# Bidirectional gated DeltaNet encoder: k and q of one chunk as one stationary matrix, and the layouts that follow

## The chip, the cores and the metric

The kernel runs on one core of one Trainium2 chip. The metric is the device time of one execution in microseconds, from the chip. One more execution was recorded by the hardware profiler; its times are those of the profile below.

## The reference, cut to what matters

One encoder layer of width 2048 over two sequences of 256 tokens in float32: h + W_out [ neighbourhood attention, 8 heads; bidirectional gated DeltaNet, 8 heads ](RMSNorm(h)), then a SwiGLU block, then a last RMSNorm. The change is in the DeltaNet heads. A sequence is cut into four chunks of 64 tokens, and a state S (128x128) runs over the chunks, once forward and once backward:

```python
def step(S, inp):
    q_i, k_i, u_i, w_i, g_i, qk_i = inp
    v_new = u_i - jnp.einsum('bhcd,bhde->bhce', w_i, S)
    o = jnp.einsum('bhcd,bhde->bhce', q_i * jnp.exp(g_i)[..., None], S) \
        + jnp.einsum('bhcs,bhse->bhce', qk_i, v_new)
    g_last = g_i[..., -1]
    S = S * jnp.exp(g_last)[..., None, None] + jnp.einsum(
        'bhcd,bhce->bhde', k_i * jnp.exp(g_last[..., None] - g_i)[..., None], v_new)
    return S, o
...
o = o_fwd + o_bwd
o = o * lax.rsqrt(jnp.mean(o * o, axis=-1, keepdims=True) + RMS_EPS) * norm_w.astype(jnp.float32)
```

u and w come from a triangular solve inside the chunk. The kernel writes a step with one matrix for each chunk and direction: r = v - exp(g) (k S), n = U r (U is the solved matrix), o = exp(g) (q S) + QK n, and S' = S exp(g_last) + kd' n, with kd the k rows scaled by their decay.

## The kernel before, in words

Both sequences lie side by side as 512 columns. All large products are 128x128 by 128x512. Weights are split into a high and a low part (load_w, L143 to L150: SP loads w_raw at L146 into one of three buffers, ScalarE makes w_hi at L138, VectorE w_lo at L139), and each product is three matmuls (mm3). half_gemm (L197 on) does eight such triples with one weight load and, after every second triple (six large matmuls, a "pump"), advances the generators in two lists, chains and side. These generators hold everything else: convolutions, attention, the lanes and the recurrence. `yield from pause(n)` lets n pumps pass. Matmuls and transposes are kept in program order; the other engines' instructions are put in order by a scheduler.

The DeltaNet heads pass through these steps:

- **k and q** (loop over 8 heads, L616 to L635): projection, convolution and silu give kq, [128 dims, k or q, 512 tokens]. POOL stores it as s_kq (L634), and the products k k and q k of each chunk as s_gram.
- **lanes** (L502 to L614): the 128 (direction, chunk, head, sequence) combinations lie on 128 partitions, W is solved on VectorE (L590, L592), the scaled matrices are made (L604, L607), and POOL stores them as s_uq in eight stores of 512 KB (L612). row_factors (L526 to L552) transposes the per-token factors and ScalarE copies them into tables (L545, L548, L551): scs for kd, egk for r, egq for os, rqs for the last norm.
- **open_recurrence** (L738 to L749) opens the pool dr in the space of the lanes, and POOL clears four uq tiles (L746).
- **fetch** (L755 to L765) loads for one head s_kq on SP (L759, tile kq) and four pieces of s_uq on POOL (L762), into block-diagonal 128x128 matrices: forward in rows and columns 0 to 63, backward in the others, one for each sequence.
- **prepare** (L767 to L789) transposes v and k on TensorE into token rows, and VectorE scales k to kd (L786).
- **recur** (L791 to L859): one generator for a head, two together for a pair. Four stages; in stage st the forward direction does chunk st and the backward one chunk 3 - st. A stage has these blocks on TensorE, for both heads of the pair one after the other:
  - S,kq (stages 1 to 3): k and q of a chunk, 64 stationary columns each, times S: eight products of 128x64 by 128x128 a head. VectorE makes r (L815, 128 partitions, two a head); ScalarE makes os from the q part (L822), VectorE in stage 2 (L820).
  - r,uq (dvn,uq in stage 0): two products of 128x128 by 128x128 a head; ScalarE copies the result to n (L829).
  - n,kd and the update of S (L849), in stages 0 to 2; then O, eight 64x64 products a pair, into two PSUM tiles that stay for the whole pair (n,uq in the profile).
  - S_GAP, R_GAP and N_GAP (3, 2 and 2 pumps) lie between them.
- **finish_pair** (L874 to L912): os plus O (L871), the norm, transposes back, the product with the gate (yo, L909) and the split into dmix (L142), which goes into the W_out projection.

The names in the profile: kkq is the lanes' big tile, ev_* are evacuated projections, cacc is the convolution's sum, dvT its result, dvn v in token rows.

Of the kernel before, what the change touches and what calls it, by code (L numbers as in the profile page):

```python
# [18 lines left out]
P = 128  # L19
# [3 lines left out]
H = 8  # L23
# [51 lines left out]
def hybrid_encoder(ctx: ExitStack, tc: tile.TileContext, xT, w_in, w_ba, w_out, w_gate,  # L75
# [51 lines left out]
    s_kq = dp.tile([H, P, 2, T], F32, name="s_kq")  # L127
# [277 lines left out]
    scs, egk = tab[:, 0], tab[:, 1]  # L405
    egq = wk.tile([P, 8, H], F32, tag="egq", name="egq")
    rqs = wk.tile([P, 2, 2, H], F32, tag="rqs", name="rqs")
# [94 lines left out]
    def lanes():  # L502
# [23 lines left out]
        def row_factors():  # L526
            _, rq = norms(qq, "nq")
            yield
            rqd = vec("rqd", 2 * C)
            for i in range(2):  # L530
                ts(rqd[:, i * C:i * C + C], rq, QSCALE, None, ALU.mult)
            egd = vec("egd", 4 * C)
            for i in range(2):
                stt(egd[:, i * C:i * C + C], eg, -1.0, rk, ALU.mult, ALU.mult)
                nc.vector.tensor_copy(egd[:, (2 + i) * C:(3 + i) * C], eg)
            ps = sm_tile()
            mm(ps[:, :P], ones, dg, start=True, stop=True)
            nc.scalar.copy(egl, ps[:, :P])
            yield
            ps = sm_tile()  # L540
            for i, v in enumerate((kd, egd[:, :2 * C], egd[:, 2 * C:], rqd)):
                transpose(ps[:, i * P:i * P + P], v, ident)
            p2 = ps[:, :2 * P].rearrange("p (i l) -> p i l", i=2)
            for (hf, st), l0 in LN.items():
                nc.scalar.copy(tab[half[hf], :, st], p2[half[hf], :, l0:l0 + 16])  # L545
            qs = ps[:, 2 * P:].rearrange("p (k h b) -> p k h b", h=H, b=NB)
            for b in range(NB):
                nc.scalar.copy(egq[half[b]], qs[half[b], :8, :, b])  # L548
                for pp in range(2):
                    ks = slice(8, 12, 3) if pp == 0 else slice(9, 11)  # L550
                    nc.scalar.copy(rqs[half[b], pp], qs[half[b], ks, :, b])  # L551
            yield  # L552
# [63 lines left out]
    for h in range(H):  # L616
# [17 lines left out]
        nc.gpsimd.dma_start(s_kq[h], kq)  # L634
# [103 lines left out]
    def open_recurrence():  # L738
# [4 lines left out]
        UQ = []  # L743
        for i in range(4):
            u = dr.tile([P, 4, 2, P], F32, tag=f"uq{i}", name=f"uq{i}")
            nc.gpsimd.memset(u, 0.0)  # L746
            UQ.append(u)
# [7 lines left out]
    def fetch(h):  # L755

        uq = state["UQ"][2 * (h % 2):2 * (h % 2) + 2]
        kq = wk.tile([P, 2, T], F32, tag="kq", bufs=2, name="kq2")
        nc.sync.dma_start(kq, s_kq[h])  # L759
        for b in range(NB):  # L760
            for hf in range(2):
                nc.gpsimd.dma_start(  # L762
                    uq[b][half[hf], :, :, hf * C:hf * C + C].rearrange("s i w c -> s (i w) c"),
                    s_uq[h * NB + b, hf].rearrange("s i w c -> s (i w) c"))
        fetched[h] = uq, kq  # L765

    def prepare(h, vT):  # L767
# [6 lines left out]
        uq, kq = fetched[h]  # L774
        yield from pause(3 + h % 2)
        pv, pk = sm_tile(), sm_tile()
        for t, u in ((pv, vT), (pk, kq[:, 0])):
            for i in range(4):
                transpose(t[:, i * P:i * P + P], u[:, i * P:i * P + P], ident)
# [3 lines left out]
        pk4 = pk.rearrange("p (b q d) -> p b q d", b=NB, q=2)  # L783
        for st in range(3):
            pp = 0 if st in (0, 3) else 1
            tt(kd[:, st], pk4[:, :, pp],  # L786
               scs[:, st, h * NB:h * NB + NB, None].broadcast_to([P, NB, P]), ALU.mult)
        prepared[h] = (uq, kq, vn, kd)
        yield  # L789

    def recur(h, O):  # L791
        dr = state["dr"]
        uq, kq, vn, kd = prepared[h]
        os_ = na.tile([P, 2, NB, P], F32, tag="bias", bufs=2, name="os")
        S = None
        for st in range(4):
            pp = 0 if st in (0, 3) else 1

            dirs = (0, 1) if st < 2 else (1, 0)
            if S is None:  # L800
                rv = vn[:, :, pp]
            else:
                yield from pause(S_GAP)

                pks = sm_tile().rearrange("p (w b e) -> p w b e", w=2, b=NB)
                for w in range(2):
                    for hf in range(2):
                        for b in range(NB):
                            c0 = b * L + pp * P + hf * C
                            to = pks[half[b], 1, hf] if w else pks[half[hf], 0, b]  # L810
                            mm(to, kq[:, w, c0:c0 + C], S[:, dirs[hf], b], start=True, stop=True)
                l0 = h * NB
                rv = dr.tile([P, NB, P], F32, tag=f"r{h % 2}", name="r")
                for b in range(NB):
                    stt(rv[:, b], pks[:, 0, b], egk[:, st, l0 + b:l0 + b + 1], vn[:, b, pp],  # L815
                        ALU.mult, ALU.add)
                for hf in range(2):
                    eq = egq[:, LN[hf, st] // 16, h:h + 1]
                    if st == 2:
                        stt(os_[:, pp, hf], pks[:, 1, hf], eq, os_[:, pp, hf], ALU.mult, ALU.add)  # L820
                    else:
                        act(out=os_[:, pp, hf], in_=pks[:, 1, hf], func=AF.Copy, scale=eq)  # L822
                yield from pause(R_GAP)
            pn = sm_tile()
            pn3 = pn.rearrange("p (w b e) -> p w b e", w=2, b=NB)[:, 0]
            for b in range(NB):
                mm(pn3[:, b], uq[b][:, st, 0], rv[:, b], start=True, stop=True)
            n = dr.tile([P, NB, P], F32, tag=f"n{h % 2}", name="n")
            nc.scalar.copy(n, pn3)  # L829
            yield from pause(N_GAP)  # L830
            if st < 3:
                pS = [None, None]
                for hf in range(2):
                    t = sm_tile() if hf else pg.tile([P, T], F32, tag="g", name="ps_s")
                    pS[dirs[hf]] = t[:, :2 * P].rearrange("p (b e) -> p b e", b=NB)
                for b in range(NB):
                    for hf in range(2):
                        mm(pS[dirs[hf]][:, b], kd[half[hf], st, b], n[half[hf], b],
                           start=True, stop=True)
                Sn = dr.tile([P, 2, NB, P], F32, tag=f"S{h % 2}", bufs=2, name="S")  # L840
                if S is None:
                    for d in range(2):
                        nc.scalar.copy(Sn[:, d], pS[d])
                else:
                    for d in range(2):
                        ch = st if d == 0 else 3 - st
                        for b in range(NB):
                            lane = d * 64 + ch * 16 + h * NB + b
                            stt(Sn[:, d, b], S[:, d, b], egl[:, lane:lane + 1], pS[d][:, b],  # L849
                                ALU.mult, ALU.add)  # L850
                S = Sn
                yield LEVEL
            for b in range(NB):
                for hf in range(2):
                    mm(O[hf][half[b], h % 2, pp], uq[b][half[hf], st, 1, hf * C:hf * C + C],
                       n[half[hf], b], start=(st == 0 and h % 2 == 0), stop=(st > 1),
                       skip_group_check=True)
        traced.add(h)
        outputs[h] = os_  # L859

    def recur_pair(h):
        while not {h, h + 1} <= set(prepared):
            yield
        yield from pause(CORE_START)
        O = [pso.tile([P, T], F32, tag=f"o{hf}", name="ps_o")
             .rearrange("p (i q e) -> p i q e", i=2, q=2) for hf in range(2)]
        yield from together(recur(h, O), recur(h + 1, O))
        for i in range(2):
            for hf in range(2):
                os_ = outputs[h + i][:, :, hf]  # L870
                tt(os_, os_, O[hf][:, i], ALU.add)  # L871
        side.append(finish_pair(h))

    def finish_pair(h):  # L874
# [4 lines left out]
        for i in range(2):  # L879
            for pp in (1, 0):  # L880
                for hf in range(2):
                    act(out=yo[:, :P], in_=outputs[h + i][:, pp, hf], func=AF.Square,
                        scale=rqs[:, pp, hf, h + i:h + i + 1], accum_out=ssq[:, i, pp, hf:hf + 1])
# [4 lines left out]
        tt(ssq, rs, rqs[:, :, :, h:h + 2].rearrange("p q f i -> p i q f"), ALU.mult)  # L888
# [9 lines left out]
        for i in range(2):  # L898
            po = sm_tile()
            to = po.rearrange("p (b q f c) -> p q f b c", b=NB, q=2, f=2)  # L900
            for pp in range(2):
                for hf in range(2):
                    transpose(to[:, pp, hf], outputs[h + i][:, pp, hf], ident)
            pos.append(po.rearrange("p (b q t) -> p b q t", b=NB, q=2))
        for i in range(2):
            if i:
                yo = na.tile([P, T], F32, tag="pT", name="yo")
            for pp in range(2):
                tt(ranged(yo, pp), pos[i][:, :, pp].rearrange("p b (c t) -> p b c t", c=2),  # L909
                   ranged(gate[h + i], pp), ALU.mult)  # L910
# [554 lines left out]
```

## Time and profile before

| | us |
|---|---|
| median of 3 runs | 2249.19 (2248.0 to 2249.99) |
| the profiled execution | 2248.75 |
| its span, first to last instruction | 2246.9 |
| TensorE busy | 2234.0 |
| VectorE busy | 1775.8 |
| ScalarE busy | 1032.1 |
| POOL busy | 237.0 |
| S,kq, first to last start | 541.7 to 765.1 |
| s_kq stores, first to last | 66.1 to 206.0 |
| s_uq stores, first to last issue | 477.5 to 487.3 |
| s_uq stores, median from issue to landing | 23.4 |

The mean granted TensorE clock was 0.998 of full speed. In the rows, PE is TensorE's matmuls, DVE VectorE, ACT ScalarE, POOL GpSimd, SPq the instructions of SP's queue (its DMA issues). A matmul's duration is longer than the distance to the next, since they are pipelined; what a block costs is read from starts. "[0.17 <-X]" is idle time of the engine ahead of the row and what ended it. Queue q1 carries SP's transfers, q0 those of POOL.

### The profile page before, as it was taken

How to read it: one execution, taken by the hardware profiler on the slowest of the kernel's cores; microseconds unless marked ns; L12 is line 12 of the kernel's file. 1: busy time of each engine (PE TensorE's matmuls, PEld its weight loads, DVE VectorE, ACT ScalarE, POOL GpSimd, SP SyncE). 2: the span in 40 equal slices, each digit the busy share in tenths (PEclk: the TensorE clock that was granted, in tenths of full speed). 3: DMA queues.
4: the chain of work that ended last, by engine and by line, in shares of the span. 5: the costliest groups of instructions: out<-in, count | busy, mean ns of one | idle time of the engine just before them, and what ended most of it. 6: DMA issues, size and time to landing. Idle time of an engine off the chain costs nothing.

```text
span 2246.9 us, 32727 instructions
## 1 busy us (share of the span) xinstructions
PE 2234.0 (99%) x12436; PEld 1911.2 (85%) x12436; DVE 1775.8 (79%) x2726; ACT 1032.1 (46%) x1552; POOL 237.0 (11%) x370
## 2 busy tenths in 40 slices
PE   9999999999999999999999999999999999999998
PEld 7888888888888888888888888888888888888888
DVE  7954799974556637888888888888888798898966
ACT  6664433333434326644444444444444464444435
POOL 1321000010000010110110111101110001001010
PEclk9999999999999999999999999999999999999999
DMA  5344322354333555778777777877777467667682
GB/s 208 132 141 144 111 97 96 98 146 135 104 104 113 189 186 188 202 201 215 199 206 198 207 195 195 216 197 211 198 201 188 150 181 208 176 178 205 176 207 84
DMA packets 112542, 381.21 MB, mean 170 GB/s; under 512 B 14049, under 2 KB 14641, under 8 KB 112129
## 3 DMA queue, kind: packets, MB, share of 16 engines
q1 hardware_dynamic: 77552, 266.25, 35.2%
q0 software_dynamic: 33680, 110.78, 23.8%
q8 instruction: 98, 1.61, 0.3%
q10 hardware_dynamic: 1152, 2.10, 0.3%
q14 instruction: 60, 0.48, 0.1%
HBM read 343.66 MB, written 35.41 MB: 169 GB/s over the span
## 4 chain that ended last, share of the span: by engine, by line
PE 94%; DVE 4%; DMA 1%; issue 1%; ACT 0%; POOL 0%; SPq 0%; DVEq 0%; POOLq 0%
PE ps_g L87 35%; PE ps_c L87 14%; PE ps_d L87 14%; PE ps_a L87 14%; PE ps_s L87 7%; PE ps_b L87 7%; DVE prod L590 1%; PE ps_s L90 1%; DVE W L592 1%; DMA kkq<-s_gram 1%; DVE w_lo L139 1%; PE ps_o L87 0%; PE ps_e L87 0%; DMA x_raw<-in_xT_dram 0%; DVE kkq L568 0%
## 5 line engine op out<-in xcount | busy, mean ns | idle before, releaser
L87 PE MATMUL ps_g<-xhi,w_hi 128*128 128x512 f32 x880 | 351.6, 400 | 0.2 <-DVE S L849 0.2
L87 PE MATMUL ps_g<-xhi,w_lo 128*128 128x512 f32 x880 | 343.4, 390 | 0.8 <-DVE w_lo L139 0.8
L87 PE MATMUL ps_g<-xlo,w_hi 128*128 128x512 f32 x880 | 343.1, 390 | 0.4 <-DVE xlo L257 0.3
L138 ACT ACTIVATE w_hi<-w_raw 128x1024 fp32r<-128x1024 f32 x164 | 173.4, 1058 | 280.2 <-PE ps_g L87 210.6
L138 ACT ACTIVATE w_hi<-b 128x1024 fp32r<-128x1024 f32 (+1 forms) x180 | 185.7, 1032 | 238.4 <-issue 119.6
L139 DVE TENSOR_TENSOR w_lo<-w_raw,w_hi 128x1024 fp32r<-128x1024 f32 x164 | 200.4, 1222 | 109.3 <-ACT w_hi L138 108.9
L138 ACT ACTIVATE w_hi<-w_first 128x1024 fp32r<-128x1024 f32 (+1 forms) x180 | 185.3, 1029 | 180.7 <-PE ps_c L87 90.9
L139 DVE TENSOR_TENSOR w_lo<-w_first,w_hi 128x1024 fp32r<-128x1024 f32 (+1 forms) x180 | 213.7, 1187 | 60.1 <-ACT w_hi L138 56.5
L139 DVE TENSOR_TENSOR w_lo<-b,w_hi 128x1024 fp32r<-128x1024 f32 (+1 forms) x180 | 212.8, 1182 | 7.6 <-ACT w_hi L138 7.1
L87 PEld LDWEIGHTS ps_g<-xhi,w_hi 128*128 128x128 f32 x880 | 165.3, 188 | 38.2 <-issue 5.0
L87 PEld LDWEIGHTS ps_g<-xhi,w_lo 128*128 128x128 f32 x880 | 165.2, 188 | 36.9 <-DVE w_lo L139 1.2
L87 PEld LDWEIGHTS ps_g<-xlo,w_hi 128*128 128x128 f32 x880 | 165.4, 188 | 33.5 <-DVE xlo L257 1.1
L87 PE MATMUL ps_d<-xc,w_hi 128*128 128x512 f32 x704 | 175.1, 391 | 0.0
L87 PE MATMUL ps_c<-xc,w_hi 128*128 128x512 f32 x704 | 175.1, 391 | 0.0
L87 PE MATMUL ps_a<-xc,w_hi 128*128 128x512 f32 x696 | 173.1, 391 | 0.0
L87 PEld LDWEIGHTS ps_c<-xc,w_hi 128*128 128x128 f32 x704 | 129.4, 188 | 25.0
L87 PEld LDWEIGHTS ps_d<-xc,w_hi 128*128 128x128 f32 x704 | 129.3, 188 | 25.0
L87 PEld LDWEIGHTS ps_a<-xc,w_hi 128*128 128x128 f32 x696 | 127.9, 188 | 24.8
L138 ACT ACTIVATE w_hi<-w_second 128x1024 fp32r<-128x1024 f32 (+1 forms) x60 | 61.9, 1032 | 93.2 <-DVE ga L1159 50.2
L87 PE MATMUL ps_d<-xc,w_lo 128*128 128x256 f32 x704 | 98.5, 283 | 0.0
L87 PE MATMUL ps_c<-xc,w_lo 128*128 128x256 f32 x704 | 98.5, 283 | 0.0
L87 PE MATMUL ps_a<-xc,w_lo 128*128 128x256 f32 x696 | 97.4, 283 | 0.0
(391 smaller groups left out, 4194.2 us busy)
## 6 DMA issues: line engine op xcount, KB each, us to landing
w_raw<-in_w_in_dram SPq DMA_DIRECT2D x108, 512.0 KB, 3.4
b<-in_w_gate_dram SPq DMA_DIRECT2D x66, 512.0 KB, 4.2
b<-in_w_up_dram SPq DMA_DIRECT2D x66, 512.0 KB, 4.8
b<-in_w_group_dram SPq DMA_DIRECT2D x48, 448.0 KB, 4.1
w_raw<-in_w_out_dram SPq DMA_DIRECT2D x32, 512.0 KB, 3.7
w_raw<-in_w_down_dram SPq DMA_DIRECT2D x24, 512.0 KB, 4.3
w_second<-in_w_gate_dram SPq DMA_DIRECT2D x22, 512.0 KB, 7.2
w_first<-in_w_gate_dram SPq DMA_DIRECT2D x22, 512.0 KB, 4.5
```

The lines of the kernel that those rows point to most:

```text
L87: pin(nc.tensor.matmul(*a, **k))
L90: pin(nc.tensor.transpose(*a))
L138: act(out=hi, in_=src, func=AF.Copy)
L139: tt(lo, src, r32(hi), ALU.subtract)
L590: stt(pv, W[:, s0:s1, s0:c], ndm[:, c:c + 1], kkq[:, c, 0, None, s0:c].broadcast_to([P, n, j]), ALU.mult, ALU.mult)
L592: nc.vector.tensor_reduce(W[:, s0:s1, c], pv, AX.X, ALU.add)
```

## The change

- s_kq is stored with k and q of one chunk side by side, in the order k,q for one half and q,k for the other, so that a chunk gives 128 stationary columns. k is stored once more, by chunk and sequence, as s_k. A head has six POOL stores (pieces of 64 numbers) where it had one.
- fetch loads s_kq as before and s_k as a further tile kn (256 KB, SP). The transposes of prepare read kn.
- uq holds 64x64 matrices and needs no zeros: two tiles instead of four, no memsets. Each head has eight POOL loads of 64x4x64 instead of four of 64x8x64: those that r,uq reads (L773) and those that O reads (L774).
- recur and recur_pair become one generator for both heads. S,kq is four products a head with 128 stationary columns; r,uq is four 64x64 products a head (eight a pair); n and O are laid out by half or sequence instead of head. Where the blocks stand between the large matmuls does not change.
- Since the factors now differ by half of the partitions, r is eight operations of 64 partitions a pair and stage instead of four of 128, os eight instead of four, yo four a head instead of two, and row_factors has 32 copies instead of 14.

The diff, cut to its core:

```diff
-    s_kq = dp.tile([H, P, 2, T], F32, name="s_kq")
+    s_kq = dp.tile([H, P, 4, 2, 2, C], F32, name="s_kq")
+    s_k = dp.tile([H, P, 4, NB, C], F32, name="s_k")
...
-        nc.gpsimd.dma_start(s_kq[h], kq)
+        k5 = kq.rearrange("p w (n f c) -> p w n f c", f=2, c=C)
+        for w in range(2):
+            for f in range(2):
+                nc.gpsimd.dma_start(s_kq[h, :, :, f, w ^ f], k5[:, w, :, f])
+        for b in range(NB):
+            nc.gpsimd.dma_start(s_k[h, :, :, b], kq[:, 0, b * L:b * L + L]
+                                .rearrange("p (n c) -> p n c", c=C))
...
-        for i in range(4):
-            u = dr.tile([P, 4, 2, P], F32, tag=f"uq{i}", name=f"uq{i}")
-            nc.gpsimd.memset(u, 0.0)
-            UQ.append(u)
+        UQ = [dr.tile([P, 2, 4, 2, C], F32, tag=f"uq{i}", name=f"uq{i}") for i in range(2)]
...
-        nc.sync.dma_start(kq, s_kq[h])
+        nc.sync.dma_start(kq.rearrange("p n f c -> p (n f c)"),
+                          s_kq[h].rearrange("p n f w c -> p (n f w c)"))
+        nc.sync.dma_start(kn, s_k[h].rearrange("p n b c -> p (n b c)"))
         for b in range(NB):
             for hf in range(2):
-                nc.gpsimd.dma_start(
-                    uq[b][half[hf], :, :, hf * C:hf * C + C].rearrange("s i w c -> s (i w) c"),
-                    s_uq[h * NB + b, hf].rearrange("s i w c -> s (i w) c"))
+                u = s_uq[h * NB + b, hf]
+                nc.gpsimd.dma_start(uq[half[hf], 0, :, b], u[:, :, 0])
+                nc.gpsimd.dma_start(uq[half[b], 1, :, hf], u[:, :, 1])
...
-                            mm(to, kq[:, w, c0:c0 + C], S[:, dirs[hf], b], start=True, stop=True)
+                            mm(pk[:, hf, b], kq[i][:, 2 * b + pp, hf], S[i][:, dirs[hf], b],
+                               start=True, stop=True)
...
-                for b in range(NB):
-                    stt(rv[:, b], pks[:, 0, b], egk[:, st, l0 + b:l0 + b + 1], vn[:, b, pp],
-                        ALU.mult, ALU.add)
+                        for b in range(NB):
+                            stt(rv[i][k, b], pks[i][k, hf, b], egk[k, st, l0 + b:l0 + b + 1],
+                                vn[i][k, b, pp], ALU.mult, ALU.add)
...
-            for b in range(NB):
-                mm(pn3[:, b], uq[b][:, st, 0], rv[:, b], start=True, stop=True)
+            for i in range(2):
+                for b in range(NB):
+                    for hf in range(2):
+                        mm(pn[hf][half[b], i], uq[i][half[hf], 0, st, b], rv[i][half[hf], b],
+                           start=True, stop=True)
...
             for (hf, st), l0 in LN.items():
-                nc.scalar.copy(tab[half[hf], :, st], p2[half[hf], :, l0:l0 + 16])
-            qs = ps[:, 2 * P:].rearrange("p (k h b) -> p k h b", h=H, b=NB)
-            for b in range(NB):
-                nc.scalar.copy(egq[half[b]], qs[half[b], :8, :, b])
+                ot = half[1 - hf]
+                nc.scalar.copy(egk[half[hf], st], p3[half[hf], 1, l0:l0 + 16])
+                nc.scalar.copy(egq[ot, st], p3[ot, 2, l0:l0 + 16])
+                if st < 3:
+                    for b in range(NB):
+                        nc.scalar.copy(scs[half[b], st, hf], p3[half[b], 0, l0 + b:l0 + 16:NB])
...
-                tt(ranged(yo, pp), pos[i][:, :, pp].rearrange("p b (c t) -> p b c t", c=2),
-                   ranged(gate[h + i], pp), ALU.mult)
+                for c in range(2):
+                    tt(ranged(yo, pp)[:, :, c], pos[i][:, :, pp, 1 - c],
+                       ranged(gate[h + i], pp)[:, :, c], ALU.mult)
```

Three places show how the change moves instructions. The first is SP's queue, from the weight loads of the first projections (w_raw) to the loads for the second head pair. Before:

```order
14 L146 DMA w_raw<-in_w_in_dram 128x1024 x32
15 L759 DMA kq_4385<-s_kq 128x1024
16 L146 DMA w_raw<-in_w_in_dram 128x1024 x4
17 L759 DMA kq_4391<-s_kq 128x1024
18 L146 DMA w_raw<-in_w_in_dram 128x1024 x56
19 L759 DMA kq_5206<-s_kq 128x1024
20 L759 DMA kq_5212<-s_kq 128x1024
```

And after:

```order
14 L147 DMA w_raw<-in_w_in_dram 128x1024 x32
15 L767 DMA kq_4438<-s_kq 128x1024
16 L147 DMA w_raw<-in_w_in_dram 128x1024 x4
17 L767 DMA kq_4450<-s_kq 128x1024
18 L147 DMA w_raw<-in_w_in_dram 128x1024 x42
19 L769 DMA kn<-s_k 128x512 x2
20 L147 DMA w_raw<-in_w_in_dram 128x1024 x8
21 L769 DMA kn<-s_k 128x512
22 L147 DMA w_raw<-in_w_in_dram 128x1024
23 L769 DMA kn<-s_k 128x512
```

The first pair's two kn loads stand ahead of the 79th weight load of this kind, which is the one issued at 484.01 in the profile of before. The second pair's stand eight and nine loads later.

The second is VectorE in stage 3 of the second head pair, where the convolution's steps (cacc) of a later head lie between the r's. Before, r,uq at 647.26 waits for the last of these r's:

```order
744 L307 TENSOR_TENSOR ev_xi<-ps_g,rstd 128x512
745 L139 TENSOR_TENSOR w_lo<-w_raw,w_hi 128x1024
746 L357 SCALAR_TENSOR_TENSOR cacc<-ev_xi,cw,cacc 128x2x254
747 L815 SCALAR_TENSOR_TENSOR r<-ps_s,tab,dvn 128x128
748 L357 SCALAR_TENSOR_TENSOR cacc<-ev_xi,cw,cacc 128x2x255
749 L815 SCALAR_TENSOR_TENSOR r<-ps_s,tab,dvn 128x128
750 L357 SCALAR_TENSOR_TENSOR cacc<-ev_xi,cw,cacc 128x2x255
751 L815 SCALAR_TENSOR_TENSOR r<-ps_s,tab,dvn 128x128
752 L357 SCALAR_TENSOR_TENSOR cacc<-ev_xi,cw,cacc 128x2x254
753 L815 SCALAR_TENSOR_TENSOR r<-ps_s,tab,dvn 128x128
754 L139 TENSOR_TENSOR w_lo<-w_raw,w_hi 128x1024
```

And after:

```order
741 L140 TENSOR_TENSOR w_lo<-w_raw,w_hi 128x1024
742 L358 SCALAR_TENSOR_TENSOR cacc<-ev_xi,cw,cacc 128x2x254
743 L831 SCALAR_TENSOR_TENSOR r<-ps_s,tab,dvn 64x128
744 L358 SCALAR_TENSOR_TENSOR cacc<-ev_xi,cw,cacc 128x2x255
745 L831 SCALAR_TENSOR_TENSOR r<-ps_s,tab,dvn 64x128
746 L358 SCALAR_TENSOR_TENSOR cacc<-ev_xi,cw,cacc 128x2x255
747 L831 SCALAR_TENSOR_TENSOR r<-ps_s,tab,dvn 64x128
748 L358 SCALAR_TENSOR_TENSOR cacc<-ev_xi,cw,cacc 128x2x254
749 L831 SCALAR_TENSOR_TENSOR r<-ps_s,tab,dvn 64x128 x5
750 L140 TENSOR_TENSOR w_lo<-w_raw,w_hi 128x1024
```

The same four convolution steps stand ahead of the last r, and four more r's.

The third is VectorE in stage 1 of the fourth pair, where finish_pair of the third (yo, dmix) and the split of the attention's output (nml) lie around the r's. Before:

```order
826 L909 TENSOR_TENSOR yo<-ps_s,ev_vn 128x2x2x64
827 L909 TENSOR_TENSOR yo<-ps_s,ev_vn 128x2x128
828 L139 TENSOR_TENSOR nml<-nml,nmh 128x512 x2
829 L142 SCALAR_TENSOR_TENSOR dmix<-yo,dnw,dmix 128x512
830 L815 SCALAR_TENSOR_TENSOR r<-ps_s,tab,dvn 128x128
831 L909 TENSOR_TENSOR yo<-ps_s,ev_s_5950 128x2x2x64
832 L909 TENSOR_TENSOR yo<-ps_s,ev_s_5950 128x2x128
833 L815 SCALAR_TENSOR_TENSOR r<-ps_s,tab,dvn 128x128 x3
834 L142 SCALAR_TENSOR_TENSOR dmix<-yo,dnw,dmix 128x512
```

And after:

```order
820 L926 TENSOR_TENSOR yo<-ps_s,ev_vn 128x2x64 x4
821 L140 TENSOR_TENSOR nml<-nml,nmh 128x512 x2
822 L143 SCALAR_TENSOR_TENSOR dmix<-yo,dnw,dmix 128x512
823 L831 SCALAR_TENSOR_TENSOR r<-ps_s,tab,dvn 64x128
824 L926 TENSOR_TENSOR yo<-ps_s,ev_s_6083 128x2x64 x4
825 L831 SCALAR_TENSOR_TENSOR r<-ps_s,tab,dvn 64x128 x6
826 L143 SCALAR_TENSOR_TENSOR dmix<-yo,dnw,dmix 128x512
827 L831 SCALAR_TENSOR_TENSOR r<-ps_s,tab,dvn 64x128
```

Both yo pairs become four operations each, and the second dmix now stands ahead of the last r.

More of the change, by code (lines that the diff above doesn't have):

```diff
@@ L773, in prepare @@
             fetch(h)
-        uq, kq = fetched[h]
+        uq, kq, kn = fetched[h]
         yield from pause(3 + h % 2)
         pv, pk = sm_tile(), sm_tile()
-        for t, u in ((pv, vT), (pk, kq[:, 0])):
+        for t, u in ((pv, vT), (pk, kn)):
             for i in range(4):
@@ L864, in recur_pair @@
         yield from pause(CORE_START)
-        O = [pso.tile([P, T], F32, tag=f"o{hf}", name="ps_o")
-             .rearrange("p (i q e) -> p i q e", i=2, q=2) for hf in range(2)]
-        yield from together(recur(h, O), recur(h + 1, O))
-        for i in range(2):
-            for hf in range(2):
-                os_ = outputs[h + i][:, :, hf]
-                tt(os_, os_, O[hf][:, i], ALU.add)
+        dr = state["dr"]
+        uq, kq, vn, kd = zip(prepared[h], prepared[h + 1])
+        O = [pso.tile([P, T], F32, tag=f"o{b}", name="ps_o")
+             .rearrange("p (i q e) -> p i q e", i=2, q=2) for b in range(NB)]
@@ L872, in recur_pair @@
+        for i in range(2):
+            traced.add(h + i)
+            outputs[h + i] = os_[i]
+            for b in range(NB):
+                o = os_[i][:, :, b]
+                tt(o, o, O[b][:, i], ALU.add)
         side.append(finish_pair(h))
@@ L880, in finish_pair @@
             for pp in (1, 0):
-                for hf in range(2):
-                    act(out=yo[:, :P], in_=outputs[h + i][:, pp, hf], func=AF.Square,
-                        scale=rqs[:, pp, hf, h + i:h + i + 1], accum_out=ssq[:, i, pp, hf:hf + 1])
+                for b in range(NB):
+                    l0 = (h + i) * NB + b
+                    act(out=yo[:, :P], in_=outputs[h + i][:, pp, b], func=AF.Square,
+                        scale=rqs[:, pp, l0:l0 + 1], accum_out=ssq[:, i, pp, b:b + 1])
         yield
@@ L887, in finish_pair @@
         newton_rsqrt(rs, ssq, dr)
-        tt(ssq, rs, rqs[:, :, :, h:h + 2].rearrange("p q f i -> p i q f"), ALU.mult)
+        tt(ssq, rs, rqs[:, :, h * NB:(h + 2) * NB].rearrange("p q (i b) -> p i q b", i=2), ALU.mult)
         for i in range(2):
@@ L898, in finish_pair @@
         for i in range(2):
-            po = sm_tile()
-            to = po.rearrange("p (b q f c) -> p q f b c", b=NB, q=2, f=2)
+            po = sm_tile().rearrange("p (b q t) -> p b q t", b=NB, q=2)
             for pp in range(2):
-                for hf in range(2):
-                    transpose(to[:, pp, hf], outputs[h + i][:, pp, hf], ident)
-            pos.append(po.rearrange("p (b q t) -> p b q t", b=NB, q=2))
+                for b in range(NB):
+                    transpose(po[:, b, pp], outputs[h + i][:, pp, b], ident)
+            pos.append(po.rearrange("p b q (c t) -> p b q c t", c=2))
         for i in range(2):
```

152 lines of the change are left out of this document (78 added, 74 removed).

## The prediction

> **What bounds the kernel now.** The page comes first: busy times, then the chain of work that ended last.
>
> ```profile
> span 2246.9 us, 32727 instructions
> ...
> PE 2234.0 (99%) x12436; PEld 1911.2 (85%) x12436; DVE 1775.8 (79%) x2726; ACT 1032.1 (46%) x1552; POOL 237.0 (11%) x370
> ...
> PE 94%; DVE 4%; DMA 1%; issue 1%; ACT 0%; POOL 0%; SPq 0%; DVEq 0%; POOLq 0%
> ```
>
> TensorE is busy for 99% of the span and is 94% of the chain. So what the change takes from PE's own sequence shows in the time at once, and what it adds elsewhere costs only where PE comes to wait for it. The profiled execution took 2248.75 us, 1.85 more than its span and 0.44 less than the median of 2249.19. All terms are added to 2248.75; at the end 0.44 is put back.
>
> The next view is PE's timeline in the first head pair's recurrence. Columns: start, duration, engine, line, operation, tiles, shapes.
>
> ```profile
> 546.13 0.39 PE L87 MATMUL ps_g<-xlo,w_hi 128*128 128x512 f32 x1
> 546.36 0.39 PE L87 MATMUL ps_g<-xhi,w_lo 128*128 128x512 f32 x1
> 546.59 1.05 PE L87 MATMUL ps_s<-r,uq 128*128 128x128 f32 x8
> 547.39 0.48 PE L87 MATMUL ps_g<-xhi,w_hi 128*128 128x512 f32 x1
> 547.71 0.39 PE L87 MATMUL ps_g<-xlo,w_hi 128*128 128x512 f32 x1
> ...
> 556.01 0.39 PE L87 MATMUL ps_g<-xhi,w_lo 128*128 128x512 f32 x1
> 556.33 2.02 PE L87 MATMUL ps_s<-S,kq 128*64 128x128 f32 x32
> ...
> 558.61 0.40 PE L87 MATMUL ps_g<-xlo,w_hi 128*128 128x512 f32 x1
> ```
>
> Large matmuls start 0.23 us apart. A block of small ones costs the time from the last large start ahead of it to the second large start behind it, less two such steps (0.46): r,uq of one pair and stage 547.71 - 546.36 - 0.46 = 0.89 us, S,kq 558.61 - 556.01 - 0.46 = 2.14 us. A product is two instructions here, so S,kq's 16 products take 0.134 us each, and r,uq's four take 0.223.
>
> **What PE saves.** S,kq comes in 12 pair-stages:
>
> ```profile
> L87 PE MATMUL ps_s<-S,kq x384: 272/273/324, 541.7 to 765.1; 128*64 128x128 f32 x192
> ```
>
> 384 instructions are 12 times 32. After the change each block has eight products with 128 stationary columns, the form of r,uq: 8 x 0.223 = 1.78 us. That saves 0.36 a block, 4.3 us in all. The other end is nothing, if the new block still took 2.14; I take 4.3, since r,uq has exactly the new shape (128*128, 128x128). The Trainium skill, "TensorEngine Tiling (Array Packing)", Key Properties, speaks against it: different tiles of the array may load and multiply in parallel, so two 64-column products could already run side by side, and nothing would be saved. The trace agrees in part: 0.134 is less than 0.223 but more than half of it.
>
> r,uq (with dvn,uq in stage 0) comes 16 times and becomes eight 64x64 products, which is what the block n,uq of stage 3 is now:
>
> ```profile
> 579.39 0.39 PE L87 MATMUL ps_g<-xhi,w_lo 128*128 128x512 f32 x1
> 579.71 0.67 PE L87 MATMUL ps_o<-n,uq 64*64 64x128 f32 x16
> ...
> 580.65 0.40 PE L87 MATMUL ps_g<-xlo,w_hi 128*128 128x512 f32 x1
> ```
>
> 580.65 - 579.39 - 0.46 = 0.80 against 0.89: 16 x 0.09 saves 1.4 us. n,kd, O and the transposes keep count and shape. PE's own sequence is shorter by **5.7 us**.
>
> **What DVE adds.** r becomes eight operations of 64 partitions instead of four of 128. The trace shows none of 64 partitions; bounds are the same time each (four more) and half (none more). I take the same, as the length of a row, 128 numbers, stays. Three places have little room between the last r and r,uq:
>
> ```profile
> 645.93 0.74 DVE L357 SCALAR_TENSOR_TENSOR cacc<-ev_xi,cw,cacc 128x508 f32<-128x508 f32 x1
> 646.59 0.35 DVE L815 SCALAR_TENSOR_TENSOR r<-ps_s,tab,dvn 128x128 f32<-128x128 f32 x1
> 647.26 1.05 PE L87 MATMUL ps_s<-r,uq 128*128 128x128 f32 x8
> 674.61 0.81 DVE L909 TENSOR_TENSOR yo<-ps_s,ev_zs 128x256 f32<-128x256 f32 x2
> 677.48 0.34 DVE L815 SCALAR_TENSOR_TENSOR r<-ps_s,tab,dvn 128x128 f32<-128x128 f32 x1
> 678.49 1.05 PE L87 MATMUL ps_s<-r,uq 128*128 128x128 f32 x8
> 737.75 0.86 DVE L815 SCALAR_TENSOR_TENSOR r<-ps_s,tab,dvn 128x128 f32<-128x128 f32 x3
> 738.62 0.75 DVE L142 SCALAR_TENSOR_TENSOR dmix<-yo,dnw,dmix 128x512 fp32r<-128x512 f32 x1
> 739.08 1.05 PE L87 MATMUL ps_s<-r,uq 128*128 128x128 f32 x8
> ```
>
> Three r's take 0.86, so one costs 0.26 in a row, and four more cost 1.03.
> - At 647.26 the last r ends at 646.94, 0.32 ahead. The new order has the same four convolution steps and then five r's: PE waits 0.7 us.
> - At 678.49 the room is 0.67. Besides the r's, the two yo multiplications (0.81) become four of half the length, at 0.26 each 0.2 more: 0.6 us.
> - At 739.08 the room is 0.47; yo costs 0.2 more, and dmix (about 0.67) now stands ahead of the last r: 1.03 + 0.2 + 0.67 - 0.47 = 1.4 us.
>
> Together **2.7 us**. Half-cost r's would leave 0.4; if S,kq's earlier end (0.36 at each place) is lost too because DVE was already behind, it is about 4. ScalarE's os copies stand behind the same r's, four more of them, and n behind those; but n is used two pumps (12 large matmuls, 2.8 us) after r,uq, so they add nothing. At the other nine pair-stages the r's end further ahead of r,uq and are taken as free.
>
> **What SP adds.** The two kn loads of the first pair (256 KB each) stand in SP's queue directly ahead of a weight load. They need space that W holds until L607 ends:
>
> ```profile
> 478.36 0.33 SPq L146 DMA_DIRECT2D w_raw<-in_w_in_dram  x1
> 478.95 3.77 DVE L607 TENSOR_TENSOR kkq<-W,nks 64x2048 f32<-64x2048 f32 x1
> 484.01 0.33 SPq L146 DMA_DIRECT2D w_raw<-in_w_in_dram  x1
> 501.81 1.06 ACT L138 ACTIVATE w_hi<-w_raw 128x1024 fp32r<-128x1024 f32 x1 [6.23 <-DMA w_raw<-in_w_in_dram]
> 502.90 1.23 DVE L139 TENSOR_TENSOR w_lo<-w_raw,w_hi 128x1024 fp32r<-128x1024 f32 x1 [8.57 <-ACT w_hi L138]
> 505.80 0.39 PE L87 MATMUL ps_g<-xhi,w_lo 128*128 128x512 f32 x1
> 505.88 1.06 ACT L138 ACTIVATE w_hi<-w_raw 128x1024 fp32r<-128x1024 f32 x1 [3.01 <-DMA w_raw<-in_w_in_dram]
> 509.79 1.06 ACT L138 ACTIVATE w_hi<-w_raw 128x1024 fp32r<-128x1024 f32 x1 [2.85 <-DMA w_raw<-in_w_in_dram]
> ```
>
> So they go out at about 482.8, and the load of 484.01 behind them. That load already lands only at 501.8, since the eight s_uq stores hold the DMA engines; its w_lo is done at 504.13, 1.67 us before PE takes it. The queues' view from 478 to 484.6 has this one line, and none for SP's queue q1, though a w_raw had been issued at 478.36:
>
> ```profile
> q0 software_dynamic: 123, 0.50, 84.6%
> ```
>
> So a transfer waits for whole transfers of the other queue. One turn of SP's queue then lasts 4.07 and 3.91 us (501.81 to 505.88 to 509.79). If each kn load takes a turn, the load behind is 7.98 late and PE waits 6.3 us; if only bytes count, two halves are one turn: 4.07 - 1.67 = 2.4. They may slip out at once with the load of 478.36: nothing. I take **5.0**, near the upper end, because the q0 row shows turns by transfer, and less than it, because a kn load has half the bytes. The Trainium skill, "DMA: Bandwidth & Descriptors", Queues, rings and completion order, says that each engine alternates between queue rows by whole packets of about 9 to 17 descriptors; by it the sum would be the 6.3 case.
>
> **Costs taken as nothing.** The memsets and the six stores a head stand on POOL, busy for 11%. Five more stores a head take POOL some 3.5 us, at 0.68 each, the price of the uq issues below (5.42 for eight); that idle time covers it. Were s_gram, which stands behind them on POOL, late by as much, W's recurrence (DVE's 4% of the chain) could pass it on to PE: the end for this edit is 3.5, inside the range. Eighteen more copies in row_factors (0.1 us each from L545's row of eight, below) fit into ACT's idle time behind them. Later kn loads stand ahead of weight loads too, but no s_uq stores run then. The uq loads, 16 of 0.68 instead of 8, are the nearest to costing:
>
> ```profile
> 364.97 0.86 ACT L545 COPY tab<-ps_s 64x32 f32<-64x32 f32 x8
> 369.91 1.06 ACT L138 ACTIVATE w_hi<-w_raw 128x1024 fp32r<-128x1024 f32 x1 [3.36 <-PE ps_g L87]
> 712.11 5.42 POOL L762 DMA_DIRECT2D uq<-s_uq  x8 [54.98 <-PE ps_o L87]
> DMA to landing us min/median/max: 2.8/3.3/5.6
> 723.42 1.05 PE L87 MATMUL ps_s<-dvn,uq 128*128 128x128 f32 x8
> ```
>
> Those that r,uq reads wait only for r,uq of the last stage, two pumps (2.8 us) before the O that releases the eight at 712.11 now. So the first goes at about 709; the 15th, the last needed, at 718.5, landing between 721.3 and 724.1 against 723.42. I take nothing; the end is 0.7.
>
> **Sum.** -5.7 + 2.7 + 5.0 = +2.0: 2250.75, with 0.44 back **2251.2 us**. Differences under 0.2% (4.5 us) can't be told from no change here.
>
> **Rivals.**
> - *The kn loads are hidden.* They go out with the load of 478.36. For: q1 is free again right then. Against: the q0 row. -5.7 + 2.7 = -3.0: 2246.2; with cheap r's (0.4) -5.3: 2243.9, faster.
> - *Slower: the long wait lowers the clock.* PE idles 6.3 us at about 506, and the granted clock halves for as long afterwards: 3.2 more. -5.7 + 2.7 + 6.3 + 3.2 = +6.5: 2255.7. It decides once PE's idle stretch is long enough. For: when PE stopped at 2238.2, the clock fell:
>
> ```profile
> 2232.00:2238.70 6.70, 4.85 (x35) 4.09 (x33) 3.03 (x10) 3.53 (x9) 0.00 (x0) 1.00 0.00 2
> 2238.80:2246.00 7.20, 0.00 (x0) 0.00 (x0) 4.18 (x5) 0.00 (x0) 0.00 (x0) 0.50 0.76 291
> ```
>
> (The last three columns are granted clock, DMA share and GB/s.) Against: this needs the longest turns. The Trainium skill, "TensorE: Matmul & The Clock Gate", Part 1, gives about 3.4 us for such a window; no stretch here tests it.
> - *The change doesn't do what it says.* S,kq keeps 2.14 a block: +2.0 + 4.3 = +6.3: 2255.5. Against: r,uq's row.
>
> **Chances.** Forecast 0.44 (of it 0.35 within 0.2%, 0.06 slower, 0.03 faster); kn hidden 0.28 (0.19 faster, 0.09 within); clock 0.18 and no saving 0.10, both slower. So faster 0.22, within 0.44, slower 0.34. The range reaches from the hidden kn with cheap r's to the two slow rivals and a little past: 2243.5 to 2256.5. The forecast alone, with 2.4 to 6.3 for kn, is 2248.6 to 2252.5.
>
> **What would show it.** S,kq 16 instructions, 1.78 a block; r,uq 16, 0.80; "idle before" of r,uq with DVE r as releaser near 647, 678 and 739 (times shifted); a PE wait near 506 ended by w_lo, and the w_hi of 501.81 at about 508. A PE that waits anywhere else, above all in the phase before 240 us with its many small stores, makes the prediction wrong.

## The result: 0.58% slower, 2262.14 us

The changed kernel takes 2262.14 us (median of 6 runs, 2261.29 to 2262.87), the kernel before beside it 2249.26 (6 runs): a ratio of 1.0058 with a 95% interval of 1.0045 to 1.0071. The prediction was 2251.2 with a range of 2243.5 to 2256.5. It was wrong by 11 us, and the likeliest case, no change that can be measured, did not come.

The page of the changed kernel, its first line and the line of the busy times:

```profile
span 2259.5 us, 32817 instructions
...
PE 2235.9 (99%) x12372; PEld 1908.8 (84%) x12372; DVE 1797.9 (80%) x2806; ACT 1043.8 (46%) x1602; POOL 279.8 (12%) x438
```

The span is 12.6 us longer. PE's busy time tells nothing here: matmuls at a low clock count as busy. The view that answers is PE's waits, between 500 and 790 us, with total, number and longest:

```profile
PE ps_s L87 <- ACT os L843: 3.0, 3, 1.7
PE ps_s L87 <- DVE os L841: 3.0, 3, 1.1
PE ps_g L87 <- ACT w_hi L139: 2.7, 1, 2.7
PE ps_s L87 <- issue: 2.4, 1, 2.4
PE ps_s L87 <- DVE r L831: 0.2, 1, 0.2
```

The kernel before has one wait in this stretch:

```profile
PE ps_g L87 <- DVE S L849: 0.2, 1, 0.2
```

Now there are 11.3 us, of four kinds: for os, for w_hi, for r, and one that the view puts under "issue" (it is S,kq's, at 743). The two largest rows belong to a step that the prediction priced at nothing: PE waits for **os**.

The savings did come. PE's timeline in the first pair:

```profile
546.54 0.39 PE L87 MATMUL ps_g<-xhi,w_lo 128*128 128x512 f32 x1
546.77 1.95 PE L87 MATMUL ps_s<-S,kq 128*128 128x128 f32 x16
...
548.78 0.39 PE L87 MATMUL ps_g<-xlo,w_hi 128*128 128x512 f32 x1
...
551.08 0.39 PE L87 MATMUL ps_g<-xhi,w_lo 128*128 128x512 f32 x1
551.40 0.67 PE L87 MATMUL ps_s<-r,uq 64*64 64x128 f32 x16
...
552.33 0.40 PE L87 MATMUL ps_g<-xlo,w_hi 128*128 128x512 f32 x1
```

By the same rule as before (start to start, less 0.46) S,kq costs 548.78 - 546.54 - 0.46 = 1.78 us and r,uq 552.33 - 551.08 - 0.46 = 0.79, as forecast.

The wait for w_hi, on ScalarE (w_hi), SP (kn) and PE:

```profile
481.90 3.35 SPq L769 DMA_DIRECT2D kn<-s_k  x2
486.97 1.06 ACT L139 ACTIVATE w_hi<-w_raw 128x1024 fp32r<-128x1024 f32 x1 [4.67 <-PE ps_g L87]
506.17 1.06 ACT L139 ACTIVATE w_hi<-w_raw 128x1024 fp32r<-128x1024 f32 x1 [11.47 <-DMA w_raw<-in_w_in_dram]
507.27 0.80 PE L87 MATMUL ps_g<-xhi,w_hi 128*128 128x512 f32 x1 [2.65 <-ACT w_hi L139]
```

The load ahead of it in the kernel before:

```profile
487.86 1.06 ACT L138 ACTIVATE w_hi<-w_raw 128x1024 fp32r<-128x1024 f32 x1 [4.67 <-PE ps_g L87]
```

The weight load behind the kn loads is split 19.2 us after the load ahead of it; before, it was 13.95 (487.86 to 501.81). That is 5.25 us later. And then the clock, in the windows view (after the engines' busy times come granted clock, DMA share and GB/s):

```profile
499.90:506.60 6.70, 4.72 (x21) 3.57 (x19) 0.00 (x0) 0.43 (x1) 0.00 (x0) 1.00 0.82 242
506.70:513.50 6.80, 6.19 (x14) 4.41 (x15) 3.05 (x3) 2.50 (x3) 1.85 (x3) 0.50 0.74 227
513.60:520.40 6.80, 6.80 (x37) 5.74 (x37) 4.13 (x5) 5.16 (x11) 4.88 (x9) 1.00 0.84 237
...
745.70:749.00 3.30, 3.30 (x12) 3.01 (x13) 3.29 (x11) 1.64 (x3) 0.00 (x0) 0.50 0.01 4
```

For 6.8 us behind the first long wait the clock stands at 0.50: large matmuls start 0.43 us apart there, and 0.23 apart ahead of it and behind it. The clock falls again at 745.7, behind the wait called "issue":

```profile
742.17 1.05 PE L87 MATMUL ps_s<-S,kq 128*128 128x128 f32 x8
745.59 2.03 PE L87 MATMUL ps_s<-S,kq 128*128 128x128 f32 x8 [2.37 <-issue]
```

Comparing the start of each large matmul with that of the same one in the kernel before gives the sum (at times of the kernel before): 0.9 us earlier at 505 (the first microseconds and a wait at 320 differ from run to run), 5.1 later at 508, so the kn wait with its low clock is **6.0**; 12.5 later at 769. Of these 7.4 the savings are -5.9; seven waits in r,uq are about +9.5 (6.2 idle, and some 0.4 for each block that is cut in two); the wait of S,kq at 743 is +3.9, 1.6 of it clock.

What PE waits for in r,uq is seen at stage 2 of the first pair, VectorE and then PE:

```profile
563.05 2.50 DVE L831 SCALAR_TENSOR_TENSOR r<-ps_s,tab,dvn 64x128 f32<-64x128 f32 x8
565.46 1.64 DVE L841 SCALAR_TENSOR_TENSOR os<-ps_s,tab,os 64x128 f32<-64x128 f32 x5
565.48 0.43 PE L87 MATMUL ps_s<-r,uq 64*64 64x128 f32 x2
566.85 0.66 PE L87 MATMUL ps_s<-r,uq 64*64 64x128 f32 x14 [0.94 <-DVE os L841]
```

All eight r's were done when r,uq began at 565.48. Its first product ran, the second stood until four os steps had passed. r,uq does not read os. But the small PSUM pool has three buffers: two hold the S,kq results of the two heads until r and os have read them, the third goes to the first half of n, and the second half needs the first head's S,kq buffer. The second half can't share a buffer with the first: the two halves of r,uq are different row tiles, that is, they use different halves of the array's rows. (The Trainium skill, "TensorEngine Tiling (Array Packing)", Restrictions and Gotchas, says so: different row tiles may not use one PSUM bank at the same time. No run here put them into one.) Before, the second n tile needed the same buffer, but only with the third of four products, and os of head 0, two operations, stood right behind head 0's two r's, as VectorE had them in this stage:

```profile
558.44 0.60 DVE L815 SCALAR_TENSOR_TENSOR r<-ps_s,tab,dvn 128x128 f32<-128x128 f32 x2
558.96 0.60 DVE L820 SCALAR_TENSOR_TENSOR os<-ps_s,egq,os 128x128 f32<-128x128 f32 x2
```

Now it is the second of eight products, and os, four operations a head, stands behind all eight r's.

So the theories for the experiments: **A**, the kn loads hold up the weight load, and the low clock adds to the price; **B**, r,uq waits for a PSUM buffer; **C**, S,kq's wait at 743 is for a PSUM buffer too, held by finish_pair. The rivals: the new stores and loads as a whole crowd the DMA engines; r of 64 partitions is slow on VectorE; S or kq comes late.

### The profile page after: what moved, and what is told of

Read it like the earlier page. It is cut to its first block, busy times and chain, and to the rows that moved or that the text cites. A ratio compares the mean times of both kernels' runs of the same rounds, so it can differ in the third digit from the quotient of the medians.

```text
span 2259.5 us, 32817 instructions
## 1 busy us (share of the span) xinstructions
PE 2235.9 (99%) x12372; PEld 1908.8 (84%) x12372; DVE 1797.9 (80%) x2806; ACT 1043.8 (46%) x1602; POOL 279.8 (12%) x438
## 4 chain that ended last, share of the span: by engine, by line
PE 68%; DVE 1%; ACT 0%; issue 0%; DVEq 0%
PE ps_g L87 14%; PE ps_c L87 14%; PE ps_d L87 14%; PE ps_a L87 14%; PE ps_b L87 7%; PE ps_s L87 4%; PE ps_e L87 0%; PE ps_o L87 0%; DVE aA L1366 0%; PE ps_s L90 0%; DVE r L831 0%; ACT w_hi L139 0%; ACT os L843 0%; DVE os L841 0%; DVE w_lo L140 0%
```

## Experiments

Times are compared by ratio to the kernel before on the same chip.

**e1: kn from POOL's queue, behind the s_uq stores** (first pair only).

```diff
-        nc.sync.dma_start(kn, s_k[h].rearrange("p n b c -> p (n b c)"))
+        (nc.sync if h > 1 else nc.gpsimd).dma_start(kn, s_k[h].rearrange("p n b c -> p (n b c)"))
```

> The first pair's two kn loads go out on POOL's queue behind the s_uq stores (at about 509) instead of on SP's queue ahead of a weight load. Theory A (the kn loads hold up that weight load, PE idles 2.65 us at 504.62, and the granted clock of 0.5 from 506.7 to 513.5 adds some 3.2): the idle and the low clock at 507 are gone, 5.5 to 6.3 us less than the changed kernel, about 2256. Rival (the weight load is late because of the s_uq stores and the other new transfers, whoever issues kn): w_hi still lands near 506 and the time stays at 2262.

2254.96 us, 1.0029 (1.0017 to 1.0041): 0.29% less than the changed kernel, 6.5 us. ScalarE's w_hi in e1:

```profile
487.86 1.06 ACT L139 ACTIVATE w_hi<-w_raw 128x1024 fp32r<-128x1024 f32 x1 [4.67 <-PE ps_g L87]
502.25 1.06 ACT L139 ACTIVATE w_hi<-w_raw 128x1024 fp32r<-128x1024 f32 x1 [6.67 <-DMA w_raw<-in_w_in_dram]
```

14.4 us apart instead of 19.2, and neither PE's wait at 505 nor the low clock is there. The other new transfers were all still made, so the rival falls. The 6.5 us are not the kn wait alone: S,kq's wait at 743 shrank as well, from 2.4 to 1.3 us, and no low clock follows it. By the starts of the large matmuls the profiled execution gains 6.0 us at the kn place and 2.6 at S,kq, and loses 1.4 elsewhere, most of it ahead of 500 us.

**e9: the kernel before with two extra loads** in the same place, unused, and nothing else of the change.

```diff
         nc.sync.dma_start(kq, s_kq[h])
+        if h < 2:
+            kn = state["dr"].tile([P, 2, NB, P], F32, tag=f"S{h}", bufs=2, name="kn")
+            nc.sync.dma_start(kn.rearrange("p d b e -> p (d b e)"), s_kq[h, :, 0])
```

> The kernel before, with nothing of the change but two extra loads of 256 KB (a head's k, not used) at the place in SP's queue where the change has kn. Theory A (these loads alone make the wait at 505 and what follows from it): w_hi lands 5 to 5.5 us later than before relative to the load ahead of it, PE idles 2.3 to 3.1 us, and the time is 2.5 us longer, or 5.5 to 6 where the granted clock falls: 2251 to 2255. Rival (the wait needs the rest of the change too): within 1 us of the kernel before.

2253.84 us, 1.0025 (1.0015 to 1.0034): 5.5 us for two loads of 0.5 MB together. PE's waits from 500 to 790, and ScalarE:

```profile
PE ps_g L87 <- ACT w_hi L138: 2.5, 1, 2.5
PE ps_g L87 <- DVE w_lo L139: 0.4, 1, 0.4
```

```profile
486.77 1.06 ACT L138 ACTIVATE w_hi<-w_raw 128x1024 fp32r<-128x1024 f32 x1 [4.67 <-PE ps_g L87]
505.85 1.06 ACT L138 ACTIVATE w_hi<-w_raw 128x1024 fp32r<-128x1024 f32 x1 [11.36 <-DMA w_raw<-in_w_in_dram]
```

19.1 us apart, and the clock stood at 0.50 for 3.41 us behind the wait. Theory A holds from both sides.

**e6: the two kn loads as one transfer of 512 KB.**

```diff
-        nc.sync.dma_start(kn, s_k[h].rearrange("p n b c -> p (n b c)"))
+        if h % 2 == 0:
+            nc.sync.dma_start(state["kn"], s_k[h:h + 2].rearrange("h p n b c -> p h (n b c)"))
```

> The changed kernel with the pair's two kn loads as one transfer of 512 KB at the same place of SP's queue. If a transfer takes a turn of its own behind the s_uq stores, whatever its size, the weight load behind it lands one turn earlier than in the changed kernel, w_hi at about 502 to 503.5 instead of 506.2 and PE idle under 0.5 us: 2256 to 2258. If bytes count, w_hi stays within 1 us of 506 and the time is as in the changed kernel, about 2261.

2260.89 us, 1.0057 (1.0043 to 1.0070), as the changed kernel; w_hi comes 19.6 us after the one ahead (488.17 to 507.76), PE idles 3.05 us and the clock falls. So a transfer does not take a turn of its own: one of 512 KB delays as much as two of 256 KB. This fits a price by bytes; no run changed the bytes.

**e2: another PSUM buffer for half of n**, from the pool of the large products.

```diff
-            pn = [sm_tile()[:, :2 * P].rearrange("p (i e) -> p i e", i=2) for hf in range(2)]
+            pn = [(sm_tile() if hf else pg.tile([P, T], F32, tag="g", name="ps_n"))[:, :2 * P]
+                  .rearrange("p (i e) -> p i e", i=2) for hf in range(2)]
```

> One of r,uq's two result tiles is taken from the pool of the large products instead of the pool of three that also holds the two S,kq tiles. Theory B (r,uq's second product waits for a PSUM buffer, which is free only when os has read head 0's S,kq tile; six of the seven waits in r,uq, 6.0 us idle and some 0.4 more each for starting again): these six waits go or shrink to what the last r costs, 5 to 8 us less than the changed kernel, about 2254 to 2257. Rival (r,uq waits because eight r's of 64 partitions take longer on VectorE, and os is only the last of a chain): the waits stay, now ended by r, and the time changes by less than 2 us.

2253.94 us, 1.0023 (1.0013 to 1.0032): 0.35% less than the changed kernel, 7.9 us. PE's waits from 500 to 790 in e2:

```profile
PE ps_g L87 <- ACT w_hi L139: 2.5, 1, 2.5
PE ps_s L87 <- issue: 1.4, 1, 1.4
PE ps_s L87 <- DVE r L831: 1.3, 4, 0.7
PE ps_g L87 <- DVE w_lo L140: 0.5, 1, 0.5
```

Both os rows are gone, and nothing on VectorE was made faster. 1.3 us are left to r. Theory B holds, but the 7.9 us are not the buffer's alone. In the profiled execution the wait for w_hi is nearly as long as in the changed kernel, yet the granted clock behind it stayed at 1.00:

```profile
506.70:513.50 6.80, 5.25 (x25) 4.12 (x26) 3.05 (x3) 2.87 (x3) 1.85 (x3) 1.00 0.71 226
```

By the starts of the large matmuls this execution gains 5.1 us in r,uq, 2.5 by the clock at the kn place (which costs 3.6 us here instead of 6.0) and 2.6 at S,kq, whose wait shrank to 1.4. It is the fastest of e2's ten runs, which lie between 2251.64 and 2255.03. In r,uq, 4.9 us of the gain lie at four places (565, 581, 637 and 701); at the other three (653, 686 and 751) r takes the place of os and 4.3 of 4.5 us stay.

**e3: e1 and e2 together.**

> Both edits. If A and B are both right and independent: 2247 to 2251, level with the kernel before. What is left above the sum of the savings (6 us of shorter S,kq and r,uq blocks) is then the wait of S,kq at 743 for a PSUM buffer held by finish_pair's transposes (2.4 us idle and 0.8 of low clock) and the r's at three places. If only one theory holds: 2254 to 2257.

2248.75 us, 0.9999 (0.9989 to 1.0008): level with the kernel before. A and B nearly add up: 6.5 and 7.9 us apart, 13.3 together. The 1.1 us that are missing are within the noise, and each edit alone had also shortened S,kq's wait.

**e4: e3 with the r's in one run on VectorE.**

```diff
-                            stt(rv[i][k, b], pks[i][k, hf, b], egk[k, st, l0 + b:l0 + b + 1],
-                                vn[i][k, b, pp], ALU.mult, ALU.add)
+                            with tc.high_priority(offset=R_AHEAD):
+                                stt(rv[i][k, b], pks[i][k, hf, b], egk[k, st, l0 + b:l0 + b + 1],
+                                    vn[i][k, b, pp], ALU.mult, ALU.add)
```

> The kn-and-bank kernel with the eight r's of a stage put ahead of the convolution, yo and dmix steps in VectorE's order, so that they stand in one run. Theory (what is left of r,uq's waits, at 645, 676 and 738, is VectorE's order: other work stands between the r's): the three waits go, with 3 to 4.5 us of the 4.3 that they cost there; about 2244.5 to 2245.5. Rival (PE's time at these places is set by the r's own length on VectorE, 64 partitions costing as much as 128): the waits shrink to no less than half, 2246.5 to 2248.

2245.17 us, 0.9988 (0.9979 to 0.9997), the only version whose interval lies below the kernel before, by 0.12%. VectorE at stage 3 of the second pair:

```profile
639.81 0.74 DVE L359 SCALAR_TENSOR_TENSOR cacc<-ev_xi,cw,cacc 128x508 f32<-128x508 f32 x1
640.47 2.73 DVE L833 SCALAR_TENSOR_TENSOR r<-ps_s,tab,dvn 64x128 f32<-64x128 f32 x8
643.23 2.32 DVE L359 SCALAR_TENSOR_TENSOR cacc<-ev_xi,cw,cacc 128x510 f32<-128x510 f32 x3
```

One convolution step stands ahead of the r's instead of four, and PE's waits at 645 and 676 are gone. At 736 a wait of 0.7 stays, ended by os again and not by r (one half of n still comes from the small pool), beside the one of S,kq, now 1.5. Of the 4.3 us at the three places 1.1 are left.

**e5: e3 with one of finish_pair's two transpose tiles from the large pool.**

```diff
-            po = sm_tile().rearrange("p (b q t) -> p b q t", b=NB, q=2)
+            po = (sm_tile() if i else pg.tile([P, T], F32, tag="g", name="ps_t")) \
+                .rearrange("p (b q t) -> p b q t", b=NB, q=2)
```

> The kn-and-bank kernel with one of the two tiles into which finish_pair transposes taken from the pool of the large products. Theory C (S,kq's wait at 732 is for a PSUM buffer of the small pool, held until VectorE has multiplied yo, which stands behind the split of the late nml): the 1.2 us idle go, 1 to 1.6 us less than the kn-and-bank kernel, about 2247.4. Rival (it waits for S or for kq): the idle stays.

2248.93 us, 1.0005 (0.9996 to 1.0014): no gain. S,kq no longer waits, so it was the buffer; but PE now reaches r,uq early and waits there for r, whose DVE order is unchanged, and the clock fell behind these waits (3.4 us at 739). The expectation was wrong on the time: the wait moved.

**e7: e4 and e5 together.**

> The kn-and-bank kernel with both of the last two edits (r's in one run, one transpose tile in the other pool). If the two waits are independent: 2243 to 2244, that is 5 us or 0.2% less than the kernel before. If one takes the place of the other: 2245 to 2247.

2246.67 us, 0.9993 (0.9984 to 1.0002), not better than e4: r,uq waits 2.5 us in one piece at 734, ended by os. One wait took the place of the other.

**e8: e4 with six of the eight nml parts on POOL.** In the changed kernel VectorE has this order there:

```profile
742.04 2.65 DVE L140 TENSOR_TENSOR nml<-nml,nmh 128x512 fp32r<-128x512 f32 x4 [4.48 <-ACT nmh L139]
744.61 0.88 DVE L926 TENSOR_TENSOR yo<-ps_s,ev_vn 128x128 f32<-128x128 f32 x4
```

It sits idle for 4.48 us until nml has landed and been split, and only then multiplies yo, whose PSUM buffer S,kq's second head needs (it starts at 745.59). In the kernel before, yo ended at 735.04, about 0.1 us before S,kq's second head (16 of the 32 instructions) was due:

```profile
734.07 2.23 PE L87 MATMUL ps_s<-S,kq 128*64 128x128 f32 x32
734.30 0.74 DVE L909 TENSOR_TENSOR yo<-ps_s,ev_vn 128x256 f32<-128x256 f32 x2
```

The edit:

```diff
-        split(nmh[:, h], nml[:, h], r32(nml[:, h]))
+        if h < 6:
+            act(out=nmh[:, h], in_=r32(nml[:, h]), func=AF.Copy)
+            nc.gpsimd.tensor_tensor(nml[:, h], r32(nml[:, h]), r32(nmh[:, h]), ALU.subtract)
+        else:
+            split(nmh[:, h], nml[:, h], r32(nml[:, h]))
```

> The r-first kernel with the low parts of the first six attention heads (nml) made on POOL, so that VectorE's yo no longer stands behind four of them. Theory C in its last form (S,kq's wait of 1.5 us at 730 and r,uq's of 0.7 at 735 come from VectorE, which waits in order for the nml transfer while yo keeps a PSUM buffer): both waits go, 2 to 2.8 us less than the r-first kernel, 2242 to 2243.5. Rival (the buffer is free, PE waits for S or kq, or POOL's slower steps hold up the first use of nml): the time stays or PE waits for nml instead, 2245 or more.

2248.57 us, 1.0001 (0.9992 to 1.0010). POOL and VectorE in e8:

```profile
727.03 8.37 POOL L984 TENSOR_TENSOR nml<-nml,nmh 128x512 fp32r<-128x512 f32 x6 [13.49 <-ACT nmh L983]
```

```profile
726.34 0.88 DVE L929 TENSOR_TENSOR yo<-ps_s,ev_vn 128x128 f32<-128x128 f32 x4 [2.99 <-PE ps_s L91]
730.83 1.78 DVE L144 SCALAR_TENSOR_TENSOR dmix<-yo,dnw,dmix 128x512 fp32r<-128x512 f32 x1 [3.61 <-ACT dmix L143]
732.53 1.75 DVE L141 TENSOR_TENSOR nml<-nml,nmh 128x512 fp32r<-128x512 f32 x1
734.20 2.71 DVE L833 SCALAR_TENSOR_TENSOR r<-ps_s,tab,dvn 64x128 f32<-64x128 f32 x8
```

yo starts as soon as its transposes are done and S,kq runs in one block of 16 without a wait, so theory C holds for its cause. The gain is lost again: dmix and one nml step take 1.78 and 1.75 us where they took 0.74 and 0.68, the r's come late, r,uq waits 1.9 us for r and then 2.2 for os, and the clock falls for 6.8 us. That the slow steps alone make the r's late is argued from their order, not tested. My expectation was wrong on the time.

## Why the prediction was wrong, step by step

- **PE's savings** (-5.7): right. 1.78 and 0.79 us a block are -4.3 and -1.6. The rival that S,kq saves nothing fell.
- **What DVE adds** (2.7): the step that failed. It said that "ScalarE's os copies" and n "add nothing", that "the other nine pair-stages" are free, and it priced r alone. r itself was sized rightly: 348 ns (median, 64 partitions) where it was 343. What was missed is a buffer, not an operation: os frees the PSUM tile that r,uq's second product needs, and the change put os behind all r's and the second tile at the second product. The waits of os are 6.0 us of idle at six places. Four of these are among the nine called free; there they cost 5.0 us, and e2 takes 4.9 of it away by a buffer alone. At the three places that the forecast named, its reason was right and its size too small: 4.5 us where it had 2.7. With the buffer changed, r,uq waits there for r instead (e2, e3), and only VectorE's order (e4) takes most of it away. The restart of a block that is cut, some 0.4 us, was not in the forecast.
- **What SP adds** (5.0): mechanism right, reason and size partly wrong. The weight load came 5.25 us later, between the 4.07 by bytes and the 7.98 by transfers, and e6 shows that the number of transfers does not set it: the turns by transfer that the prediction read from the q0 row are not what delays it. By the prediction's own slack of 1.67 us, 5.25 leave 3.6, and 3.6 is what the place costs in e2, where the clock stayed up. The Trainium skill's rule of whole packets ("DMA: Bandwidth & Descriptors", Queues, rings and completion order), read as one turn a transfer, doesn't agree with e6.
- **The clock** (a rival, 0.18): the low clock came, the 6.3 us of idle did not. 2.65 us were enough. Its price is 2.4 us at the kn place (6.0 less the 3.6 of e2) and 1.6 behind S,kq's wait. Rival and forecast should not have been apart: the clock also fell behind a wait of 2.37 us, so any wait of that length had a chance of it.
- **Not seen at all**: S,kq at 743, +3.9. In the kernel before, yo ended about 0.1 us before S,kq's second head needed its PSUM tile. nml landed 6.1 us after its first issue (4.0 before), and that margin was gone. Where finish_pair's tiles are left as they are, S,kq's wait follows this landing: 0.9 us at 4.6 (e6), 1.2 at 4.9 (e3), 1.5 at 5.3 (e4), 2.4 at 6.1. e8 shows the chain; why the transfer takes longer than before in every version of the change is open.

Put together, by the starts of the large matmuls:

| term, us | forecast | measured |
|---|---|---|
| PE's savings | -5.7 | -5.9 |
| r,uq at the three places named | 2.7 | 4.5 |
| r,uq at four places called free | 0 | 5.0 |
| kn loads, without the low clock | 5.0 | 3.6 |
| low clock behind the kn wait | 0 | 2.4 |
| S,kq at 743 with its low clock | 0 | 3.9 |
| sum | 2.0 | 13.5 |

The first 500 us, 0.9 shorter in the profiled execution, bring this to the 12.6 by which the span is longer.

The uq loads, the memsets, row_factors and the small stores cost nothing that the trace shows, as taken.

## What to carry to other kernels

Before moving a read, list the buffers that it frees, not only who reads its result: PE waited here for a step whose output it never uses. A load put ahead of another in a queue delays it, here by 5.1 to 5.6 us for 0.5 MB, and slack there is to be counted per place. Where PE is busy all the time, price a wait of 2 us or more twice: at little more than its length, and at about twice that, for the case that the clock falls behind it. And read what an edit gains place by place: both e1 and e2 also gained at S,kq, at which neither was aimed.

## What the runs showed of the hardware

- The granted clock falls well before 3.4 us of idle. It fell behind one wait of 2.65 us (the changed kernel) and stayed for 6.83 us; behind 1.65 in e6, for 3.41; and stayed at 1.00 behind 2.48 and 0.52 in e2 and behind 2.47 in e7. The same kn place cost 3.6 us with the clock at 1.00 (e2), 4.9 with 3.41 us of 0.50 (e9) and 6.0 with 6.83 us of it (the changed kernel). The Trainium skill, "TensorE: Matmul & The Clock Gate", Part 1, has a window of 3413 ns that runs free of the kernel; the lengths seen, 3.41 and twice that, agree, and that the same wait has two outcomes would follow from where it lies in the window. No run set that place.
- VectorE's steps of 128x512 took 1.78 and 1.75 us while POOL worked on tiles of the same size (e8), and 0.74 and 0.68 without it.
- SP loads of 0.5 MB together delayed the one behind them by 5.1 us as two transfers (e9) and by 5.6 as one (e6), while the eight s_uq stores were on the way, though weight loads of 0.5 MB each came 4.07 and 3.91 us apart there in the kernel before.
